# Ten FFN blocks with three Strassen-like pairs instead of two, B's stores on another queue, and two edits at the GLU

## The chip, the core and the metric

The kernel runs on one core of one Trainium2 chip, as one launch. The metric is the device time in microseconds (us) of one execution; the median of three runs is given, and one more execution was recorded by the hardware profiler.

## The reference

One decoder block on x of shape (1, 256, 2048), all in float32:

```python
u   = rms_norm(x)
p   = u @ w_in                       # q, k, v, ssm_in, gate_attn, gate_ssm
y_a = diff_attention(q, k, v)        # 8 heads, two softmax maps each
y_s = gelu(s5_scan(ssm_in))          # 64 groups, complex states
y_s = y_s * sigmoid(y_s @ w_glu + b_glu)
m   = sigmoid(g_a) * (y_a @ w_attn) + sigmoid(g_s) * (y_s @ w_ssm)
h   = x + rms_norm(m @ w_out)
z   = rms_norm(h)
f   = (silu(z @ w_gate) * (z @ w_up)) @ w_down     # 2048 -> 5632 -> 2048
out = h + rms_norm(f)
```

With 256 tokens the work is mostly the reading of weights and their products.

## The kernel before

A float32 product is made of three products in a rounded float32 type (fp32r): each operand is split into a high part and a low part (value minus high), and hi·hi, hi·lo and lo·hi are summed in PSUM. The tokens are two tiles of 128 (t = 0, 1). A weight matrix is read in k-tiles of 128 rows by 1024 columns: SyncE issues the load into a tile `raw`, ScalarE casts it to `hi`, VectorE subtracts to get `lo`; together this is a *split*. `ensure` emits splits up to 4 ahead of TensorE's products and loads further ahead. There are 3 + 2 buffers for hi and lo, so a buffer comes free after five sets. Nearly all vector, scalar and tensor instructions are recorded by one helper (line 41), which then puts them in a fixed order per engine; the order that results, not that of the code, is what each engine executes, in order and without overtaking.

The feed-forward part runs in blocks of 512 gate columns and 512 up columns. Block 0 is a plain block. Blocks 1 to 10 use a list `SETS`. An entry `D` is one k-tile: four partial products (P4, P5, P2, P3) into two 512-column banks, twelve matmuls of 128x512. A *quad* covers two k-tiles (k and k+1, a *pair*) by seven products instead of eight: entries `R2` (the second weight tile, 6 matmuls), `B1` (half of the first tile, 3), `T13` (two sums of weights, 6) and `T24` (two more, 6), so 21 matmuls where two `D` have 24. The sums of weights are made by `do_sums`, three VectorE subtractions: one 128x1024 (t1 and t3 together, called S13 below) and two 128x512 (t2, t4). The four loads of a pair go into one buffer, `ga[:, 1]`, and the sums into one buffer, `ga[:, 0]`. So in a trace a pair's work reads `ga<-ga` (sums) and `lo<-ga` (splits of R2, B1, T13, T24). `ensure` issues no loads of a next pair before the B1 split of the pair in hand has been emitted. The tokens' side of the seven products (sums of z) is made once by `combos` at the end of block 0. With two quads a block has 12 `D` and 2 quads, 186 matmuls.

Two other places matter. In the first part, the B matrices of the state space are made in `ga` and written to a scratch tensor `stack_b` in 12 stores of 256 KB (SyncE's queue, line 668); `fetch` (line 752) reads them back half a group at a time. GpSimd meanwhile builds tables of powers (lines 682 to 687). Where the GLU product begins, the last four gate banks of the input projection are evicted by `gs_evac` (three by ScalarE, one by VectorE), ScalarE casts y, loads an activation table, and TensorE starts on `w_glu`.

Of the kernel before, what the change touches and what calls it, by code (L numbers as in the profile page):

```python
# [14 lines left out]
ALU = mybir.AluOpType  # L15
# [74 lines left out]
def hybrid_block_kernel(  # L90
# [7 lines left out]
    nc = tc.nc  # L98
    pin = [True]
    V, A, T = (InOrder(tc, e, pin) for e in (nc.vector, nc.scalar, nc.tensor))  # L100
    G = nc.gpsimd
# [3 lines left out]
    stack_b = dram.tile([NG, 2, 3, 32, 2, 2, P], F32, name="stack_b")  # L105
# [37 lines left out]
    def big8(dtype=F32, shape=(P, 2048)):  # L143
        return b8.tile(list(shape), dtype, tag="b8", name=nm("b8"))
# [115 lines left out]
    def cap(blk, n, start=False):  # L260

        state["cap"] = None if n is None else blk.base + n
        if start:
            pin[0] = True
# [177 lines left out]
    hold = {}  # L442
# [76 lines left out]
    def prep():  # L519
# [57 lines left out]
        cs = pp.tile([P, 8, 32], F32, name="cs")  # L577
# [40 lines left out]
        for base, levels in ((0, 4), (4, 3)):  # L618
# [10 lines left out]
            for l in range(levels):  # L629
                n = 1 << l  # L630
# [20 lines left out]
        bh, bl = (ga[:, i, :, :].rearrange("p a (c o q) -> p (a c) o q", c=4, o=2) for i in range(2))  # L651
        for gg in range(NG // 2):
            ps = side()
            for e in range(2):
                g = 2 * gg + e
                for o in range(2):
                    t_ = blkB[e][o]
# [3 lines left out]
            gs = slice(2 * gg, 2 * gg + 2)  # L661
            src = ps.rearrange("p (a o q) -> p a o q", a=2, o=2)
            A.copy(bh[:, gs].bitcast(F32R), src)
            V.tensor_tensor(bl[:, gs], src, bh[:, gs], op=ALU.subtract)
            yield 0.7
        for n, t_ in enumerate((bh, bh, bl)):
            for j in range(4):
                nc.sync.dma_start(stack_b[:, j // 2, n, :, j % 2].rearrange("g q o n -> q g o n"), t_[32 * j:32 * j + 32])  # L668
                yield 0.2


    def table(hh):
# [291 lines left out]
    def scaled_copy(dst, src, sc):  # L964
        eng[0] += 1
        if eng[0] % 4:
            A.activation(dst, src, AF.Copy, scale=sc)
        else:
            V.tensor_scalar(dst, src, sc, None, op0=ALU.mult)
# [13 lines left out]
    def add(*a, **kw):  # L983
        b = Block(*a, **kw)
        if b.order is None:
            b.order = bank_order(b.nk)
        blocks.append(b)
        return b
# [24 lines left out]
    def first_load(k, r):  # L1013
# [6 lines left out]
        if k in (1, 3, 6):  # L1020
            load_x((1, 3, 6).index(k) + 1)

    tasks.append(("prep", prep()))
    add("ssm", 16, first_load, lx, proj_evac("u"), budget=1.2, ensure=x_ensure)

# [43 lines left out]
    def gs_evac(half_):  # L1069
        def f(key, accs):  # L1070
            t, c = key
            if ("gs", half_) not in hold:
                hold[("gs", half_)] = big8()
            scaled_copy(hold[("gs", half_)][:, t * 1024 + c * 512:t * 1024 + c * 512 + 512], accs[key],
                        hold["rstd"][:, t:t + 1])
        return f

    for hf in range(2):
# [2 lines left out]
    def gs_sigmoid(hf):  # L1081
        for c in (0, 1024):
            g = hold[("gs", hf)][:, c:c + 1024]
            A.activation(g, g, AF.Sigmoid)
# [21 lines left out]
    def glu_evac(key, accs):  # L1106
# [13 lines left out]
    add("glu", 8, load_std(w_glu, 0), None, glu_evac, mm=glu_mm, alloc=glu_alloc, pre=glu_pre,  # L1120
        order=[[(k, mt, 0) for mt in range(8)] for k in range(6)]
        + [[(k, mt, 0) for mt in (2 * b, 2 * b + 1) for k in (6, 7)] for b in range(4)], budget=0.6,
        before={2: lambda: gs_sigmoid(0), 4: lambda: gs_sigmoid(1), 6: lambda: cap(glu, 10, True)})
    glu = blocks[-1]

    def ly2(k, t):
# [37 lines left out]
    for hf in range(2):  # L1164
        add(f"ws{hf}", 8, load_std(w_ws, 1024 * hf), ly2, ws_evac(hf), budget=0.8, post=ws_post(hf),
            before={0: lambda: cap(glu, None), 1: unpin} if hf == 0 else None)
# [68 lines left out]
    def zf(t):  # L1235
        return ga[:, t].rearrange("p a (k n) -> p (a k) n", n=P)

    def combos(cb):

        if cb == 0:  # L1240
            cs = big8(F32R, (P, 2, 4, 2, P))
            hold["cs"], hold["cd"] = (cs[:, 0], cs[:, 1]), [big8(F32R, (P, 16, P)) for _ in range(2)]
        z0, z1 = zf(0), zf(1)
        n = 2 if cb % 2 else 4
        k0, k1, k2 = 4 * cb, 4 * cb + 2, 4 * cb + 3
        tt = V.tensor_tensor
        (ch, cl), (dh, dl) = hold["cs"], hold["cd"]
        tt(z1[:, k0:k0 + n], z0[:, k0:k0 + n], z1[:, k0:k0 + n], op=ALU.subtract)
        parts = [(z1[:, k0:k0 + n], dh[:, k0:k0 + n], dl[:, k0:k0 + n])]
        if n == 2:  # L1250
            tt(z1[:, k2], z1[:, k1], z1[:, k2], op=ALU.add)
            tt(z1[:, k1], z0[:, k1], z1[:, k1], op=ALU.subtract)
            tt(z0[:, k1], z1[:, k2], z0[:, k1], op=ALU.subtract)
            tt(z0[:, k2], z0[:, k2], z0[:, k1], op=ALU.subtract)
            parts += [(z1[:, k1:k1 + 2], ch[:, 0:2, cb // 2], cl[:, 0:2, cb // 2]),
                      (z0[:, k1:k1 + 2], ch[:, 2:4, cb // 2], cl[:, 2:4, cb // 2])]
        for src, h, l in parts:
            A.copy(h, src)
            tt(l, src, h.bitcast(F32), op=ALU.subtract)

    def h_transpose(t, cb):
        ps = side4()
        for j in range(4):
            k = 4 * cb + j
            transpose(ps[:, j * P:(j + 1) * P], hx[t][:, k * P:(k + 1) * P])
        z = zf(t)[:, 4 * cb:4 * cb + 4, :]
        V.tensor_tensor(z, ps.rearrange("p (a b) -> p a b", a=4),
                        wffn[:, 4 * cb:4 * cb + 4].unsqueeze(2).broadcast_to([P, 4, P]), op=ALU.mult)
        zs[t, cb] = z
# [26 lines left out]
    def norm2():  # L1296
# [9 lines left out]
        before={12: lambda: cap(wo1, 17, True), 13: lambda: cap(wo1, 17, True), 16: lambda: cap(wo1, 18), 17: lambda: h_transpose(0, 0)})  # L1306
# [6 lines left out]
    def load_ffn(b):  # L1313
        def f(k, r):
            for w, c0 in ((w_g, 0), (w_u, 512)):
                nc.sync.dma_start(r[:, :, c0:c0 + 512],
                                  w[k * P:(k + r.shape[1]) * P, b * 512:(b + 1) * 512].rearrange("(a p) c -> p a c", p=P))
        return f
# [33 lines left out]

    quad = lambda k: [(kind, k) for kind in ("R2", "B1", "T13", "T24")]
    plain = lambda *ks: [("D", k) for k in ks]
    SETS = plain(0, 1, 2, 3, 4) + quad(6) + plain(5, 8, 9, 10) + quad(14) + plain(11, 12, 13)
    USES = dict(D=(("P4", 0), ("P5", 1), ("P2", 0), ("P3", 1)), R2=(("P2", 0), ("P3", 1)), B1=(("P1", 0),),
                T13=(("P7", 1), ("P5", 0)), T24=(("P6", 0), ("P4", 1)))

    def s_mm(m, accs, h, l, first, last):
        n, key, c = m  # L1360
        kind, k = SETS[n]
        (ch, cl), (dh, dl) = hold["cs"], hold["cd"]
        z = lambda k_, t: tuple(zT[i][:, k_, t * P:(t + 1) * P] for i in "hl")
        q = k // 8
        if kind == "D":
            xh, xl = dict(P4=z(k, 1), P5=z(k, 1), P2=z(k, 0), P3=(dh[:, k], dl[:, k]))[key]
        elif key in ("P1", "P2", "P4"):
            xh, xl = dict(P1=z(k, 0), P2=z(k + 1, 0), P4=z(k + 1, 1))[key]
        else:
            i = dict(P7=0, P5=1, P6=2, P3=3)[key]  # L1370
            xh, xl = ch[:, i, q], cl[:, i, q]
        ps, sl = accs[key], slice(c * 512, c * 512 + 512)
        T.matmul(ps, xh, h[:, sl], start=first, stop=False)
        T.matmul(ps, xh, l[:, sl], start=False, stop=False)
        T.matmul(ps, xl, h[:, sl], start=False, stop=last)
# [17 lines left out]
    def s_evac(b):  # L1393
        def f(key, accs):
            s0, s1, X, Y = (hold["sc"][:, 512 * n:512 * n + 512] for n in range(4))
            plus = lambda o, a, k_: V.tensor_tensor(o, a, accs[k_], op=ALU.add)

            def gated(t, g, u):
                A.activation(g, g, AF.Silu, scale=hold["rstd2"][:, t:t + 1])
                V.scalar_tensor_tensor(g, u, hold["rstd2"][:, t:t + 1], g, op0=ALU.mult, op1=ALU.mult)  # L1400
                hid[(b, t)] = g
            if key == "P1":
                A.copy(s0, accs["P1"])
            elif key == "P6":
                plus(X, s0, "P6")
                plus(Y, X, "P7")
            elif key == "P4":
                plus(s1, Y, "P4")
            elif key == "P5":
                plus(X, X, "P5")  # L1410
                plus(Y, Y, "P5")
                gated(1, s1, Y)
            elif key == "P2":
                plus(s0, s0, "P2")
            elif key == "P3":
                plus(X, X, "P3")
                gated(0, s0, X)
                tasks.append((f"hid{b}", hid_t(b)))
        return f

    every = [[(n, key, c) for key, c in USES[kind]] for n, (kind, _) in enumerate(SETS)]
    s_order = [st[:3] for st in every[:3]] + [[st[3] for st in every[:3]]] + every[3:-2]
    s_order.append([st[i] for i in range(4) for st in every[-2:]])
    for b in range(1, NB):
        add(f"ffn{b}", len(SETS), load_ffn(b), None, s_evac(b), budget=0.6, mm=s_mm, alloc=s_alloc(b), order=s_order)
        blocks[-1].sets = SETS
        blocks[-1].akey = lambda m: m[1]
# [108 lines left out]
    def dn_weights():  # L1536
# [5 lines left out]
             before={8: dn_weights})  # L1542
# [39 lines left out]
```

## Time and profile before

| | us |
|---|---|
| median of three runs | 1394.79 |
| lowest, highest | 1393.06, 1396.41 |
| the profiled execution | 1398.8 |
| its span, first to last instruction | 1397.0 |
| TensorE busy in it | 1356.9 (97%) |
| VectorE busy | 1009.5 (72%) |
| ScalarE busy | 722.6 (52%) |
| GpSimd busy | 168.3 (12%) |

The mean granted TensorE clock was 0.983 of full speed. Busy shares are means over stages of different kinds. An instruction's length on VectorE overlaps the next by about 0.08 us, which is seen where two rows follow each other without idle time.

### The profile page before, as it was taken

What the parts mean: (1) busy time and instruction counts of PE and PEld (TensorE: products, weight loads), DVE (VectorE), ACT (ScalarE), POOL (GpSimd) and SP (SyncE); (2) the same over time, 40 slices, a digit from 0 to 9 for tenths busy, and PEclk for the clock granted to TensorE, in tenths of its full rate; (3) what the DMA queues carried; (4) which work ended last, traced back from release to release, by engine and by line L of the source; (5) the groups of instructions that cost most, each with busy time, mean ns of one, the idle gap of its engine ahead of it and who ended that gap; (6) DMA issues with size and microseconds to landing.
All of it is one profiled execution on the core that took longest, in us unless ns stands there. A gap on an engine that the chain in (4) does not pass through costs nothing.

```text
span 1397.0 us, 17778 instructions
## 1 busy us (share of the span) xinstructions
PE 1356.9 (97%) x6307; PEld 1104.5 (79%) x6307; DVE 1009.5 (72%) x1316; ACT 722.6 (52%) x1079; POOL 168.3 (12%) x187
## 2 busy tenths in 40 slices
PE   7999999999999989999999999999999999999997
PEld 6887777777777778888788888888888878888885
DVE  4954999868999956645976777767868676555555
ACT  3646545687545454544574555545555455444443
POOL 3090344302244100000000000000000000000001
PEclk8999999999999989999999999999999999999999
DMA  8678666544566556656566656566565566555551
GB/s 244 200 225 253 212 190 186 153 136 143 176 177 187 167 175 227 223 187 197 166 193 207 211 154 229 172 200 211 175 210 189 180 248 228 189 201 180 197 181 60
DMA packets 103577, 266.72 MB, mean 191 GB/s; under 512 B 11488, under 2 KB 18480, under 8 KB 100352
## 3 DMA queue, kind: packets, MB, share of 16 engines
q1 hardware_dynamic: 102272, 260.09, 58.5%
q10 hardware_dynamic: 608, 4.20, 0.8%
q0 software_dynamic: 608, 1.30, 0.4%
q8 instruction: 49, 0.80, 0.2%
q14 instruction: 40, 0.33, 0.1%
HBM read 257.16 MB, written 8.39 MB: 190 GB/s over the span
## 4 chain that ended last, share of the span: by engine, by line
issue 53%; PE 25%; DVE 13%; POOL 3%; ACT 3%; DMA 2%; SPq 1%; POOLq 0%; DVEq 0%; ACTq 0%
PE acc L41 23%; DVE lo L41 4%; PE side L41 2%; DVE ssB L41 2%; DVE ssD L41 2%; DVE ssA L41 2%; DVE ssC L41 1%; ACT hi L41 1%; DMA b<-in_x_dram 1%; SPq L668 1%; DVE ga L41 1%; DVE sim L41 1%; DVE b L41 1%; POOL tabS L685 1%; DVE sre L41 0%
## 5 line engine op out<-in xcount | busy, mean ns | idle before, releaser
L41 DVE TENSOR_TENSOR lo<-raw,hi 128x1024 fp32r<-128x1024 f32 (+1 forms) x385 | 473.6, 1240 | 163.7 <-ACT hi L41 163.0
L41 ACT CAST hi<-raw 128x1024 fp32r<-128x1024 f32 (+1 forms) x384 | 398.0, 1050 | 318.3 <-PE acc L41 220.1
L41 PE MATMUL acc<-hi,b 128*128 128x512 f32 x596 | 209.2, 394 | 0.4 <-DVE b L41 0.3
L41 PE MATMUL acc<-lo,xT_h 128*128 128x512 f32 x512 | 205.0, 404 | 2.6 <-DVE lo L41 2.5
L41 PE MATMUL acc<-hi,xT_l 128*128 128x512 f32 x512 | 202.4, 399 | 0.0
L41 PE MATMUL acc<-hi,xT_h 128*128 128x512 f32 x512 | 164.1, 406 | 5.3 <-ACT hi L41 3.5
L41 PEld LDWEIGHTS acc<-hi,b 128*128 128x128 f32 x596 | 112.4, 189 | 24.9 <-issue 0.8
L41 PEld LDWEIGHTS acc<-lo,xT_h 128*128 128x128 f32 x512 | 98.5, 193 | 28.1 <-DVE lo L41 5.1
L41 PEld LDWEIGHTS acc<-hi,xT_h 128*128 128x128 f32 x512 | 97.2, 193 | 28.4 <-ACT hi L41 6.2
L41 PE MATMUL acc<-lo,b 128*128 128x512 f32 x298 | 117.4, 394 | 2.1 <-DVE lo L41 2.1
L41 DVE TENSOR_TENSOR lo<-ga,hi 128x1024 fp32r<-128x1024 f32 x80 | 84.6, 1087 | 47.0 <-ACT hi L41 47.0
L41 ACT CAST hi<-ga 128x1024 fp32r<-128x1024 f32 x80 | 72.7, 943 | 82.1 <-PE acc L41 71.5
L41 PEld LDWEIGHTS acc<-hi,xT_l 128*128 128x128 f32 x512 | 98.3, 192 | 19.6
L41 PE MATMUL acc<-lo,zT_h 128*128 128x512 f32 x274 | 105.8, 392 | 0.4 <-DVE lo L41 0.4
L41 PE MATMUL acc<-hi,zT_l 128*128 128x512 f32 x274 | 105.1, 390 | 0.0
L41 PE MATMUL acc<-hi,zT_h 128*128 128x512 f32 x274 | 95.4, 393 | 0.2 <-ACT zT_h L41 0.2
L41 DVE TENSOR_TENSOR ga<-ga 128x512 f32<-128x512 f32 (+4 forms) x85 | 60.5, 716 | 35.4 <-DMA ga<-in_w_ffn_gate_dram 32.2
L439 POOL TENSOR_TENSOR rstdf<-rstdfm,half 128x1 f32<-128x1 f32 x2 | 1.1, 547 | 675.3 <-DVE rstdfm L41 675.3
L41 PE MATMUL side<-lo,zT_h 128*128 128x512 f32 x210 | 82.1, 391 | 0.0
L41 PE MATMUL side<-hi,zT_l 128*128 128x512 f32 x210 | 81.8, 389 | 0.0
L41 PE MATMUL side<-hi,zT_h 128*128 128x512 f32 x210 | 77.7, 389 | 0.0
L41 DVE TENSOR_TENSOR lo<-b,hi 128x1024 fp32r<-128x1024 f32 x40 | 49.0, 1225 | 39.0 <-ACT hi L41 39.0
(230 smaller groups left out, 2326.7 us busy)
## 6 DMA issues: line engine op xcount, KB each, us to landing
raw<-in_w_in_dram SPq DMA_DIRECT2D x127, 512.0 KB, 4.2
raw<-in_w_ffn_gate_dram SPq DMA_DIRECT2D x136, 256.0 KB, 3.7
raw<-in_w_ffn_up_dram SPq DMA_DIRECT2D x136, 256.0 KB, 4.0
raw<-in_w_ffn_down_dram SPq DMA_DIRECT2D x48, 512.0 KB, 4.3
b<-in_w_ffn_down_dram SPq DMA_DIRECT2D x20, 1024.0 KB, 4.9
raw<-in_w_out_dram SPq DMA_DIRECT2D x32, 512.0 KB, 4.1
ga<-in_w_ffn_gate_dram SPq DMA_DIRECT2D x40, 256.0 KB, 3.7
ga<-in_w_ffn_up_dram SPq DMA_DIRECT2D x40, 256.0 KB, 3.0
```

Source lines behind the costliest of these rows:

```text
L41: ins = f(*a, **kw)
L439: G.tensor_tensor(r, ms, half[:, :n], op=ALU.pow)
L668: nc.sync.dma_start(stack_b[:, j // 2, n, :, j % 2].rearrange("g q o n -> q g o n"), t_[32 * j:32 * j + 32])
L685: G.tensor_tensor(up(tss), hi(sa), lo(cb), op=ALU.mult)
```

## The change

Four parts. `SETS` has a third quad (k = 10), and the plain sets stand elsewhere; the tokens' sums for it are made by `combos` and kept in unused slots of another tile. The 12 stores of B go out on GpSimd's queue, in another sequence. `gs_evac` lets VectorE evict three of the last four gate banks. A `cap` delays the splits of `w_glu` in the first steps of the GLU block.

```diff
--- before.py
+++ after.py
@@ -663,10 +663,12 @@
             A.copy(bh[:, gs].bitcast(F32R), src)
             V.tensor_tensor(bl[:, gs], src, bh[:, gs], op=ALU.subtract)
             yield 0.7
-        for n, t_ in enumerate((bh, bh, bl)):
-            for j in range(4):
-                nc.sync.dma_start(stack_b[:, j // 2, n, :, j % 2].rearrange("g q o n -> q g o n"), t_[32 * j:32 * j + 32])
-                yield 0.2
+        for hf in range(2):
+            for n, t_ in enumerate((bh, bh, bl)):
+                for j in (0, 1):
+                    r = 32 * (2 * hf + j)
+                    G.dma_start(stack_b[:, hf, n, :, j].rearrange("g q o n -> q g o n"), t_[r:r + 32])
+                    yield 0.2
 
 
     def table(hh):
@@ -1071,8 +1073,12 @@
             t, c = key
             if ("gs", half_) not in hold:
                 hold[("gs", half_)] = big8()
-            scaled_copy(hold[("gs", half_)][:, t * 1024 + c * 512:t * 1024 + c * 512 + 512], accs[key],
-                        hold["rstd"][:, t:t + 1])
+            dst, sc = hold[("gs", half_)][:, t * 1024 + c * 512:t * 1024 + c * 512 + 512], hold["rstd"][:, t:t + 1]
+            if half_ == 1 and key != (0, 0):
+
+                V.tensor_scalar(dst, accs[key], sc, None, op0=ALU.mult)
+            else:
+                scaled_copy(dst, accs[key], sc)
         return f
 
     for hf in range(2):
@@ -1120,7 +1126,8 @@
     add("glu", 8, load_std(w_glu, 0), None, glu_evac, mm=glu_mm, alloc=glu_alloc, pre=glu_pre,
         order=[[(k, mt, 0) for mt in range(8)] for k in range(6)]
         + [[(k, mt, 0) for mt in (2 * b, 2 * b + 1) for k in (6, 7)] for b in range(4)], budget=0.6,
-        before={2: lambda: gs_sigmoid(0), 4: lambda: gs_sigmoid(1), 6: lambda: cap(glu, 10, True)})
+        before={0: lambda: cap(glu, 1), 1: lambda: cap(glu, 3), 2: lambda: (cap(glu, None), gs_sigmoid(0)),
+                4: lambda: gs_sigmoid(1), 6: lambda: cap(glu, 10, True)})
     glu = blocks[-1]
 
     def ly2(k, t):
@@ -1235,13 +1242,19 @@
     def zf(t):
         return ga[:, t].rearrange("p a (k n) -> p (a k) n", n=P)
 
+    def sums_of(k, i, n, part):
+
+        if k == 10:
+            return hold["cd"][part][:, (6, 7, 14, 15)[i]:(6, 7, 14, 15)[i] + n]
+        return hold["cs"][part][:, i:i + n, k // 8]
+
     def combos(cb):
 
         if cb == 0:
             cs = big8(F32R, (P, 2, 4, 2, P))
             hold["cs"], hold["cd"] = (cs[:, 0], cs[:, 1]), [big8(F32R, (P, 16, P)) for _ in range(2)]
         z0, z1 = zf(0), zf(1)
-        n = 2 if cb % 2 else 4
+        n = 2 if cb else 4
         k0, k1, k2 = 4 * cb, 4 * cb + 2, 4 * cb + 3
         tt = V.tensor_tensor
         (ch, cl), (dh, dl) = hold["cs"], hold["cd"]
@@ -1252,8 +1265,8 @@
             tt(z1[:, k1], z0[:, k1], z1[:, k1], op=ALU.subtract)
             tt(z0[:, k1], z1[:, k2], z0[:, k1], op=ALU.subtract)
             tt(z0[:, k2], z0[:, k2], z0[:, k1], op=ALU.subtract)
-            parts += [(z1[:, k1:k1 + 2], ch[:, 0:2, cb // 2], cl[:, 0:2, cb // 2]),
-                      (z0[:, k1:k1 + 2], ch[:, 2:4, cb // 2], cl[:, 2:4, cb // 2])]
+            for i, src in ((0, z1), (2, z0)):
+                parts.append((src[:, k1:k1 + 2], sums_of(k1, i, 2, 0), sums_of(k1, i, 2, 1)))
         for src, h, l in parts:
             A.copy(h, src)
             tt(l, src, h.bitcast(F32), op=ALU.subtract)
@@ -1352,7 +1365,8 @@
 
     quad = lambda k: [(kind, k) for kind in ("R2", "B1", "T13", "T24")]
     plain = lambda *ks: [("D", k) for k in ks]
-    SETS = plain(0, 1, 2, 3, 4) + quad(6) + plain(5, 8, 9, 10) + quad(14) + plain(11, 12, 13)
+    SETS = (plain(0, 1, 2, 3) + quad(6) + plain(4, 5) + quad(10) + plain(8, 9) + quad(14)
+            + plain(12, 13))
     USES = dict(D=(("P4", 0), ("P5", 1), ("P2", 0), ("P3", 1)), R2=(("P2", 0), ("P3", 1)), B1=(("P1", 0),),
                 T13=(("P7", 1), ("P5", 0)), T24=(("P6", 0), ("P4", 1)))
 
@@ -1361,14 +1375,13 @@
         kind, k = SETS[n]
         (ch, cl), (dh, dl) = hold["cs"], hold["cd"]
         z = lambda k_, t: tuple(zT[i][:, k_, t * P:(t + 1) * P] for i in "hl")
-        q = k // 8
         if kind == "D":
             xh, xl = dict(P4=z(k, 1), P5=z(k, 1), P2=z(k, 0), P3=(dh[:, k], dl[:, k]))[key]
         elif key in ("P1", "P2", "P4"):
             xh, xl = dict(P1=z(k, 0), P2=z(k + 1, 0), P4=z(k + 1, 1))[key]
         else:
             i = dict(P7=0, P5=1, P6=2, P3=3)[key]
-            xh, xl = ch[:, i, q], cl[:, i, q]
+            xh, xl = (sums_of(k, i, 1, part)[:, 0] for part in (0, 1))
         ps, sl = accs[key], slice(c * 512, c * 512 + 512)
         T.matmul(ps, xh, h[:, sl], start=first, stop=False)
         T.matmul(ps, xh, l[:, sl], start=False, stop=False)
```

On VectorE, in one of the FFN blocks before, around the second pair (first row: the split of R2; 852 is B1, 854 T13, 856 T24; 855 is S13 of the next pair, 851, 853, 857 and 859 are t2 and t4):

```order
850 L41 TENSOR_TENSOR lo_7616<-ga,hi_7615 128x1024
851 L41 TENSOR_TENSOR ga<-ga 128x512
852 L41 TENSOR_TENSOR lo_7635<-ga,hi_7634 128x512
853 L41 TENSOR_TENSOR ga<-ga 128x512
854 L41 TENSOR_TENSOR lo_7657<-ga,hi_7656 128x1024
855 L41 TENSOR_TENSOR ga<-ga 128x1024
856 L41 TENSOR_TENSOR lo_7676<-ga,hi_7675 128x1024
857 L41 TENSOR_TENSOR ga<-ga 128x512
858 L41 TENSOR_TENSOR lo_7696<-raw_7563,hi_7695 128x1024
859 L41 TENSOR_TENSOR ga<-ga 128x512
860 L41 TENSOR_TENSOR lo_7706<-raw_7576,hi_7705 128x1024
```

S13 of the next pair stands between this pair's T13 and T24.

The same engine after, from B1 of the first pair of a block (939) through T13 and T24, S13 of the second pair (942), two plain sets, that pair's R2, B1, T13 and t4 (946 to 949), to S13 of the third pair (950):

```order
939 L41 TENSOR_TENSOR lo_8211<-ga,hi_8210 128x512
940 L41 TENSOR_TENSOR lo_8234<-ga,hi_8233 128x1024
941 L41 TENSOR_TENSOR lo_8259<-ga,hi_8258 128x1024
942 L41 TENSOR_TENSOR ga<-ga 128x1024
943 L41 TENSOR_TENSOR lo_8275<-raw_8110,hi_8274 128x1024
944 L41 TENSOR_TENSOR lo_8285<-raw_8123,hi_8284 128x1024
945 L41 TENSOR_TENSOR ga<-ga 128x512
946 L41 TENSOR_TENSOR lo_8292<-ga,hi_8291 128x1024
947 L41 TENSOR_TENSOR lo_8302<-ga,hi_8301 128x512
948 L41 TENSOR_TENSOR lo_8322<-ga,hi_8321 128x1024
949 L41 TENSOR_TENSOR ga<-ga 128x512
950 L41 TENSOR_TENSOR ga<-ga 128x1024
```

Two plain sets instead of four stand between pairs. It goes on as follows, from R2 of the third pair (954) over B1 (956), T13 and T24 to S13 of the next block's first pair (960) and the block's last plain sets (961 and 963); rows 951 to 953, left out, are two plain sets and a T24:

```order
954 L41 TENSOR_TENSOR lo_8383<-ga,hi_8382 128x1024
955 L41 TENSOR_TENSOR ga<-ga 128x512
956 L41 TENSOR_TENSOR lo_8396<-ga,hi_8395 128x512
957 L41 TENSOR_TENSOR ga<-ga 128x512
958 L41 TENSOR_TENSOR lo_8413<-ga,hi_8412 128x1024
959 L41 TENSOR_TENSOR lo_8429<-ga,hi_8428 128x1024
960 L41 TENSOR_TENSOR ga<-ga 128x1024
961 L41 TENSOR_TENSOR lo_8445<-raw_8318,hi_8444 128x1024
962 L41 TENSOR_TENSOR ga<-ga 128x512
963 L41 TENSOR_TENSOR lo_8455<-raw_8337,hi_8454 128x1024
```

On SyncE before, the stores among the weight loads:

```order
53 L349 DMA raw_1194<-in_w_in_dram 128x1024
54 L349 DMA raw_1227<-in_w_in_dram 128x1024
55 L668 DMA stack_b<-ga 32x8x256 x12
56 L349 DMA raw_1229<-in_w_in_dram 128x1024
57 L349 DMA raw_1276<-in_w_in_dram 128x1024
58 L349 DMA raw_1311<-in_w_in_dram 128x1024
59 L752 DMA bsf_1177<-stack_b 96x512
```

and on GpSimd after, where they stand between a step of the tables and the next group's first:

```order
90 L689 TENSOR_TENSOR tabS_1213<-tabS_1213,tabt_209_1214 128x2x128
91 L685 TENSOR_TENSOR tabt_243_1359<-tabs_970,tabs_942 128x256
92 L670 DMA stack_b<-ga 32x8x256 x12
93 L687 TENSOR_TENSOR tabS_1358<-tabs_970,tabc_941 128x2x128
94 L684 TENSOR_TENSOR tabC_1357<-tabc_969,tabc_941 128x2x128
```

SyncE's loads close up over the gap, and GpSimd's next table step stands behind twelve stores.

On ScalarE before, at the start of the GLU product (presig is the activation after the table load; the first cast is y's first k-tile, the next `w_glu`'s, then the gate evictions):

```order
408 L41 ACTIVATE presig<-half 128x1
409 L41 CAST b_931_4609<-b_123_726 128x256
410 L41 CAST hi_4751<-raw_4649 128x1024
411 L41 ACTIVATE b_942_4665<-acc_4308,rstdx_608 128x512
412 L41 ACTIVATE b_942_4665<-acc_4309,rstdx_608 128x512
413 L41 ACTIVATE b_942_4665<-acc_4310,rstdx_608 128x512
414 L41 CAST b_931_4609<-b_123_726 128x256 x4
```

and after:

```order
406 L41 ACTIVATE presig<-half 128x1
407 L41 CAST b_931_4609<-b_123_726 128x256
408 L41 CAST hi_4779<-raw_4649 128x1024
409 L41 ACTIVATE b_942_4665<-acc_4308,rstdx_608 128x512
410 L41 CAST b_931_4609<-b_123_726 128x256 x4
411 L41 ACTIVATE b_942_4665<-b_942_4665 128x1024 x2
```

Two evictions leave ScalarE, and y's other four casts come right behind the first.

## Rows read from the trace of the kernel before

**Rows 1.** The page: busy time and share by engine

```profile
PE 1356.9 (97%) x6307; PEld 1104.5 (79%) x6307; DVE 1009.5 (72%) x1316; ACT 722.6 (52%) x1079; POOL 168.3 (12%) x187
```

**Rows 2.** Busy time by stretch: us, engines (instructions), TensorE clock, DMA share, GB/s

```profile
130.00:140.00 10.00, 7.03 (x24) 5.28 (x23) 2.45 (x2) 4.07 (x9) 0.00 (x0) 0.76 0.98 307
...
504.00:508.00 4.00, 3.12 (x14) 3.12 (x15) 2.98 (x6) 4.00 (x9) 0.00 (x0) 0.50 0.80 268
...
855.00:897.50 42.50, 42.50 (x189) 35.03 (x188) 32.37 (x35) 21.55 (x24) 0.00 (x0) 1.00 0.57 186
700.00:712.00 12.00, 12.00 (x55) 9.91 (x53) 10.14 (x18) 10.13 (x19) 1.64 (x1) 1.00 0.70 210
```

**Rows 3.** VectorE's groups by form, 855 to 1280 us: busy, mean ns, idle before

```profile
L41 DVE TENSOR_TENSOR lo<-raw,hi 128x1024 fp32r<-128x1024 f32 x111 | 133.8, 1221 | 32.2 <-ACT hi L41 32.0
...
L41 DVE TENSOR_TENSOR ga<-ga 128x512 f32<-128x512 f32 x26 | 17.9, 687 | 0.3
L41 DVE TENSOR_TENSOR b<-b,acc 128x512 f32<-128x512 f32 x27 | 17.6, 680 | 0.0
L41 DVE TENSOR_TENSOR ga<-ga 128x1024 f32<-128x1024 f32 x13 | 15.9, 1223 | 22.2 <-DMA ga<-in_w_ffn_gate_dram 22.2
...
L41 DVE SCALAR_TENSOR_TENSOR b<-b,rstdh 128x512 f32<-128x512 f32 x14 | 10.4, 745 | 0.0
```

**Rows 4.** VectorE's waits by what ended them: total us, times, longest

```profile
DVE ga L41 <- DMA ga<-in_w_ffn_gate_dram: 32.2, 13, 4.2
```

**Rows 5.** VectorE's timeline in one FFN block: start, us, [idle before]

```profile
857.22 4.10 DVE L41 TENSOR_TENSOR lo<-ga,hi 128x1024 fp32r<-128x1024 f32 x4 [5.49 <-ACT hi L41]
861.23 2.36 DVE L41 TENSOR_TENSOR lo<-raw,hi 128x1024 fp32r<-128x1024 f32 x2
863.51 1.22 DVE L41 TENSOR_TENSOR ga<-ga 128x1024 f32<-128x1024 f32 x1
...
868.65 0.68 DVE L41 TENSOR_TENSOR lo<-ga,hi 128x512 fp32r<-128x512 f32 x1
869.25 0.68 DVE L41 TENSOR_TENSOR ga<-ga 128x512 f32<-128x512 f32 x1
...
873.94 1.23 DVE L41 TENSOR_TENSOR ga<-ga 128x1024 f32<-128x1024 f32 x1 [2.56 <-DMA ga<-in_w_ffn_gate_dram]
```

**Rows 6.** TensorE's timeline: first product on the sums' low part

```profile
862.92 0.39 PE L41 MATMUL acc<-lo,b 128*128 128x512 f32 x1
```

**Rows 7.** SyncE's queue while B is stored

```profile
117.62 11.31 SPq L668 DMA_DIRECT2D stack_b<-ga  x12
129.03 2.80 SPq L349 DMA_DIRECT2D raw<-in_w_in_dram  x3
```

**Rows 8.** ScalarE's timeline in the same stretch

```profile
134.77 1.04 ACT L41 CAST hi<-raw 128x1024 fp32r<-128x1024 f32 x1 [8.95 <-DMA raw<-in_w_in_dram]
```

**Rows 9.** TensorE's timeline in the same stretch

```profile
135.87 2.07 PE L41 MATMUL acc<-hi,xT_h 128*128 128x512 f32 x4 [2.97 <-ACT hi L41]
```

**Rows 10.** GpSimd's timeline around the stores

```profile
105.49 0.63 POOL L683 TENSOR_TENSOR tabt<-tabs,tabs 128x256 f32<-128x256 f32 x1
154.98 2.67 POOL L685 TENSOR_TENSOR tabS<-tabs,tabc 128x256 f32<-128x256 f32 x1 [48.87 <-DVE ssB L41]
```

**Rows 11.** DMA issues of the first 60 us: KB, median us to landing

```profile
cn<-in_ssm_c_im_dram POOLq DMA_DIRECT2D x1, 256.0 KB, 12.6
```

**Rows 12.** ScalarE's timeline where the GLU product begins

```profile
499.18 1.99 ACT L41 CAST hi<-raw 128x1024 fp32r<-128x1024 f32 x2 [3.82 <-DMA raw<-in_w_glu_dram]
...
504.15 1.83 ACT L41 ACTIVATE b<-acc,rstdx 128x512 f32<-128x512 f32 x3
505.88 1.32 ACT L41 CAST b<-b 128x256 fp32r<-128x256 f32 x4
```

**Rows 13.** TensorE's timeline there

```profile
504.88 0.80 PE L41 MATMUL acc<-b,hi 128*128 128x256 f32 x2 [6.33 <-ACT b L41]
```

## The prediction

> **What bounds the kernel now.** I began with the busy table, where the reader is to see that TensorE is busy 97% of the span and VectorE 72% [rows 1]. Those are means. The change acts in FFN blocks 1 to 10, so next I took the stretches: a 42.5 us stretch of these blocks has TensorE busy throughout at full clock, with 189 matmuls, that is 0.225 us from start to start, and VectorE busy for 32.4 us, ScalarE for 21.6 [rows 2]. TensorE bounds there, and a matmul less is worth 0.225 us only as long as VectorE's splits arrive ahead of it. So the third view is VectorE's timeline, and the fourth its waits. They show that VectorE's margin is smaller than 72% says: its queue stands still for the loads of a pair, 13 times and 32.2 us in all [rows 4], because the first of the three sums (S13) sits at the head of the queue while splits that could run stand behind it.
>
> **The FFN blocks, TensorE's side.** Each block loses three matmuls (186 to 183): 10 × 3 × 0.225 = 6.8 us, if nothing else becomes late.
>
> **The FFN blocks, VectorE's side.** The pitch of an instruction is its mean less the 0.08 us that overlaps the next: a 128x1024 split or S13 1.22 − 0.08 = 1.14, a 128x512 subtraction 0.60, an eviction 0.60, a scaled eviction 0.67 [rows 3]. A plain set costs 1.14; a quad costs R2, T13 and T24 (3.42), B1 (0.60) and the sums (1.14 + 2 × 0.60), 6.36 together. Evictions are seven of 0.60 and two of 0.67 per block, 5.5. Before: 12 × 1.14 + 2 × 6.36 + 5.5 = 31.9 us, which agrees with the 32.4 measured. After: 10 × 1.14 + 3 × 6.36 + 5.5 = 36.0 us. TensorE needs 183 × 0.225 and some 0.7 us of transposes, 41.9. On that alone VectorE would fit in.
>
> What is added to it are the waits for loads. In the timeline, B1's split ended at 869.33 and t4 at 869.93, and the next pair's S13 started at 873.94 [rows 5]: 4.6 us after the one, 4.0 after the other. The single pair buffer cannot be refilled sooner, since these two read it last. So S13 waits for 4.6 us after the previous B1, or 4.0 after t4 if that is later, less whatever VectorE has to do in between. I go through the order after the change with that rule. Second pair: T13 and T24 lie between, 2.28 us, so it waits 2.3. Third pair: T13 and t4 come before it, and t4 directly, so it waits 4.0. Next block's first pair: after t4 come T13 and T24, so 1.7. Sum 8.0 us per block; all of it stands ahead of the next plain splits in the same queue. Checked on before, the rule gives 2.9 us (4.0 less one split) where 2.56 was measured [rows 5], so it reads a little high; 6.0 us is my low bound. Before has 32.2 us in ten blocks, 3.2 each. VectorE's block thus becomes 42 to 44 us against TensorE's 41.9: by capacity alone −0.6 to +1.4 us per block against 42.6 before.
>
> Capacity is the kinder of two bounds, as the sets aren't interchangeable: VectorE may run ahead only as far as there are buffers. At the first quad of a block its lead is small: the four splits that began at 857.22 came after 5.49 us of waiting on ScalarE's cast, which waits for a buffer, and the last of them (T24) ended at about 861.3, while TensorE first used it at 862.92 [rows 5, 6]. That is 1.6 us of lead. From there to the block's last plain set the order after the change has 17 instructions of 1.14 and 7 of 0.60, 23.6 us, and all three waits, 6.0 to 8.0: 29.6 to 31.6 us. TensorE does 3 + 6 + 6 + 24 + 21 + 24 + 21 + 12 = 117 matmuls in that stretch, 26.3 us. With a lead of 1.6 to 2.8 VectorE is late by 29.6 − 26.3 − 2.8 = 0.5 us to 31.6 − 26.3 − 1.6 = 3.7 us, once in each block, and TensorE waits for it. What is waited is not given back, because at the block's end the deferred products hold the buffers again. I take 2.4 us, a bit above the middle, as the waits go into a queue that also needs ScalarE's cast of each sum. Less the 0.7 us of matmuls a block gets longer by 1.7 us: +17 us for ten. The ends are (0.5 − 0.7) × 10 = −2 and (3.7 − 0.7) × 10 = +30.
>
> **B's stores.** Twelve issues hold SyncE's queue for 11.31 us, and the next weight load goes out at 129.03 [rows 7]. ScalarE's cast then waits 8.95 us for it [rows 8], TensorE stands 2.97 us [rows 9], and its clock falls to 0.76 in that stretch, where 24 matmuls took 7.03 us of busy time instead of 24 × 0.225 = 5.4 [rows 2]. So at most 2.97 + 1.6 = 4.6 us can be won. On the other side GpSimd is idle from 106 to 154.98 [rows 10], and there is room for the issues; but its own 256 KB loads took up to 12.6 us to land [rows 11], and the read-back of B stands in SyncE's queue ahead of later weight loads. If the stores land late, the same wait appears there: at worst the same 4.6 us again. I take −1.5, a third of what could be won.
>
> The share of the DMA engines was 0.98 in that stretch, at 307 GB/s [rows 2]: 12 stores of 256 KB are 3.1 MB, 10.2 us of that. The Trainium skill says (Trainium Kernel Development and Optimization, Key Constraints) that transfers issued from SyncE, ScalarE and GpSimd run on the same 16 engines and interleave, and that several issuers only save issue time. By that rule 11.31 us of issue would go and 10.2 us of transfer stay, and the gain would be about 1 us in place of my 1.5; the row with 0.98 agrees with it.
>
> **The GLU's start.** TensorE waits 6.33 us and starts at 504.88 [rows 13], when ScalarE's first gate eviction, begun at 504.15, is through [rows 12]. That eviction stays where it is, with the table load and the wait for the load of `w_glu` ahead of it. The two evictions that go to VectorE bring y's other four casts from 505.88 to about 504.7, but TensorE is busy without a break from 504.88 on (3.12 us of 3.12 at a granted clock of 0.50, the lower of its two levels, 1.2 GHz) [rows 2], so nobody waited for them. The later splits can bring the first ones forward by one, 1 us at most; three evictions in VectorE's row, 2 × 0.67 more, can push a low part back by 1.3. I take −0.3, with −1.2 and +1.3 as ends.
>
> **The tokens' sums.** Two casts and some six VectorE subtractions more at the end of block 0, about 2 to 3 us, where VectorE has 10.14 us of work in 12 [rows 2]. Cover is block 0's own lead; I take 0, with +2 at the other end.
>
> **Sum.** 17 − 1.5 − 0.3 + 0 = +15.2 us on the profiled execution's 1398.8, 1414.0. That execution lies 4.0 above the median of the runs, so 1410.
>
> **Rivals.** *TensorE stays the bound.* S13 may be waited for less than my rule says, as with 32.2 us in 20 pairs before (1.6 each): three pairs at 1.6 are 4.8, VectorE's block 40.8, below 41.9, and the path 28.4 against 26.3 + 2.8. Then −6.8 − 1.5 − 0.3 comes out, to −11.4 with all of the B stores' gain: 1383 to 1386, say 1386. For it speaks that the loads' wait is only reached if VectorE is ahead, and that a late VectorE waits less; against it, the small lead at each block's start.
>
> *It cancels.* VectorE's lateness is at the low end, 0.5 to 0.7 us per block, and eats the matmuls: 1398.8 − 1.5 − 0.3 ± 2 less 4.0, about 1393.
>
> *The stores on the other queue decide.* TensorE keeps its 6.8 us, but B comes back late, and SyncE stands at the read-back with weight loads behind it: no weight load can go out until the last store has landed, up to 12.6 us after its issue [rows 11]. Against the 2.97 us stop of before [rows 9] that is 9.6 us more, and 1.6 again at the low clock: 1398.8 − 6.8 + 11.2 − 4.0 = 1399. It decides from 6.8 us of added stop on. For it speaks the landing time; against it, that the read-back in SyncE's queue has moved behind more weight loads than before.
>
> **Chances and range.** Forecast 0.57 (1399 to 1428 by the ends of its terms, 1410 its middle); TensorE stays the bound 0.25; cancels 0.13; stores 0.05. A run of this kernel can tell 0.2%, about 2.8 us, from no change. The first rival is faster altogether; of the cancelling case about half is faster and half the same; the last and the forecast's cases are slower, but for a few at its low end that are the same. So faster 0.32, same 0.11, slower 0.57. The range is 1386 to 1428: up to the upper ends of the FFN term, and down to the first rival's value.
>
> **What would show it.** Right: in the FFN blocks VectorE's waits for the pair's loads grow from 32 to 60 us or more, TensorE shows idle time ended by VectorE's low parts (or ScalarE's casts of sums) once or more in each block, and a block lasts 44 us or so. Wrong: TensorE stays without gaps there and its blocks last 41.9 us. The stores' term is right if TensorE's gap at 133 us shrinks, wrong if one opens at the read-back of B. At the GLU the first product would start within 1 us of where it was, relative to the end of the input projection. A larger fall of the clock in the FFN blocks than 0.95 would make the time longer than my range.

## The result and the profile after

The changed kernel takes 1417.21 us (median; 1415.06 to 1420.61), the kernel before 1395.6 in the same comparison: ratio 1.0161, 95% interval 1.0145 to 1.0177, so 21.6 us slower. Forecast were 1410 and +15.2.

The page of the changed kernel, busy time by engine (it answers to [rows 1]):

```profile
PE 1361.3 (96%) x6277; PEld 1097.7 (77%) x6277; DVE 1050.6 (74%) x1374; ACT 737.1 (52%) x1099; POOL 175.9 (12%) x199
```

VectorE has 41 us more to do, TensorE 30 matmuls less, and yet its busy share has fallen. Where the time is: the ten FFN blocks, from the first matmul of block 1 to the last of block 10, first of before, then of the changed kernel (columns as in [rows 2]):

```profile
714.04:1149.50 435.46, 435.01 (x1958) 359.94 (x1956) 323.93 (x350) 223.32 (x255) 0.00 (x0) 1.00 0.60 196
```

```profile
713.79:1168.69 454.90, 439.81 (x1928) 355.22 (x1928) 364.65 (x400) 238.30 (x275) 0.00 (x0) 0.99 0.59 186
```

The blocks take 19.4 us longer, nearly all of the loss. TensorE is idle for 15.1 us of 454.9 where it was idle for 0.4 us before; the rest of the loss hides in matmuls that start more than 0.227 us after the one before them, while the engine counts as busy. I therefore lined up the matmuls of each trace with the program and counted, set by set, what TensorE's starts take beyond 0.2267 us each, the distance of starts where nothing is waited for. That sum is called *lost time* below: 0.1 us in before's ten blocks, 26.1 us in the changed kernel's (26.1 − 6.8 = 19.3, the difference above). Summed over the ten blocks, by place: 6.5 us in D0 to D2, 10.1 in D3, 9.2 from the second pair's T24 on (that T24 2.7, D8 2.1, D12 4.4). D3's 10.1 us lie in blocks 3, 5, 7 and 9 alone, 2.1 to 3.1 us in each. The profiled execution of before took 4.0 us more than its median, and at 50 us all the other profiles are 1.1 to 3.7 us ahead of it, so below only what is gained or lost between two places of a profile is compared.

VectorE's waits from 712 to 1161 us, changed kernel (answers to [rows 4], where the loads had 32.2 us in 13 waits):

```profile
DVE lo L41 <- ACT hi L41: 38.1, 27, 5.5
DVE ga L41 <- DMA ga<-in_w_ffn_gate_dram: 29.6, 17, 2.8
DVE b L41 <- PE side L41: 13.7, 4, 3.6
DVE ga L41 <- DMA ga<-in_w_ffn_up_dram: 3.7, 6, 1.5
```

The waits for a pair's loads are more in number, 23 instead of 14, but not longer in sum (33.3 us; before had 34.6 with the one on an up load). That contradicts my rule, though not the time.

Why the rule fails can be read at the end of block 9, VectorE in the changed kernel (t4 of the third pair, then the next block's S13):

```profile
1109.43 0.69 DVE L41 TENSOR_TENSOR ga<-ga 128x512 f32<-128x512 f32 x1
1110.27 1.23 DVE L41 TENSOR_TENSOR ga<-ga 128x1024 f32<-128x1024 f32 x1 [0.15 <-DMA ga<-in_w_ffn_up_dram]
```

S13 starts 0.15 us after t4 has ended, where the rule has 4.0. In `do_sums` t4 is the last to read the second tile's gate half, and S13 doesn't read this half, so it need not wait for the load that t4 lets go.

Two places in one block each. After t4 of the second pair, VectorE, then TensorE:

```profile
960.90 0.68 DVE L41 TENSOR_TENSOR ga<-ga 128x512 f32<-128x512 f32 x1
964.01 1.23 DVE L41 TENSOR_TENSOR ga<-ga 128x1024 f32<-128x1024 f32 x1 [2.42 <-DMA ga<-in_w_ffn_gate_dram]
965.15 1.22 DVE L41 TENSOR_TENSOR lo<-raw,hi 128x1024 fp32r<-128x1024 f32 x1
```

```profile
966.42 0.50 PE L41 MATMUL side<-lo,zT_h 128*128 128x512 f32 x1 [0.83 <-DVE lo L41]
```

S13 of the third pair waits 2.42 us at the head of the queue (the forecast had 4.0), the plain set D8 behind it is split too late, and TensorE stands 0.83 us. That is the mechanism of the forecast. D12 behind the third pair loses in the same way, behind S13 of the next block's first pair; VectorE, then TensorE, in block 8:

```profile
1066.95 1.23 DVE L41 TENSOR_TENSOR ga<-ga 128x1024 f32<-128x1024 f32 x1 [2.72 <-DMA ga<-in_w_ffn_gate_dram]
1068.09 1.22 DVE L41 TENSOR_TENSOR lo<-raw,hi 128x1024 fp32r<-128x1024 f32 x1
```

```profile
1069.37 0.50 PE L41 MATMUL side<-lo,zT_h 128*128 128x512 f32 x1 [0.90 <-DVE lo L41]
```

The other place is the entry of a block; TensorE, ScalarE and VectorE in the changed kernel at the start of block 5:

```profile
898.53 0.39 PE L41 MATMUL acc<-hi,zT_l 128*128 128x512 f32 x1
898.75 0.39 PE L41 MATMUL side<-hi,zT_h 128*128 128x512 f32 x1
...
899.89 0.39 PE L41 MATMUL side<-hi,zT_l 128*128 128x512 f32 x1
900.78 0.96 PE L41 MATMUL acc<-hi,zT_h 128*128 128x512 f32 x3 [0.50 <-ACT hi L41]
902.79 0.50 PE L41 MATMUL acc<-lo,zT_h 128*128 128x512 f32 x1 [1.05 <-DVE lo L41]
```

```profile
899.68 1.05 ACT L41 CAST hi<-raw 128x1024 fp32r<-128x1024 f32 x1 [1.98 <-PE side L41]
```

```profile
900.31 1.29 DVE L41 TENSOR_TENSOR b<-b,side 128x512 f32<-128x512 f32 x2 [3.39 <-PE side L41]
901.51 1.22 DVE L41 TENSOR_TENSOR lo<-raw,hi 128x1024 fp32r<-128x1024 f32 x1
```

Up to 898.53 these are products of the new block's D2; `side` from 898.75 to 899.89 are the last products of the old block's D12 and D13, and only they free the buffers that D3's split needs. The cast starts at 899.68, VectorE first adds a bank that the same products finished to two results (900.31), then splits (901.51), and TensorE waits 0.50 and 1.05 us. Before, the same products stand the other way round:

```profile
889.90 0.39 PE L41 MATMUL side<-hi,zT_h 128*128 128x512 f32 x1
...
891.03 0.39 PE L41 MATMUL side<-hi,zT_l 128*128 128x512 f32 x1
891.26 0.39 PE L41 MATMUL acc<-hi,zT_h 128*128 128x512 f32 x1
...
893.98 0.46 PE L41 MATMUL acc<-lo,zT_h 128*128 128x512 f32 x1
```

There the old products (`side`, 889.90 to 891.03) come ahead of D2 (891.26), D2's nine matmuls cover the split of D3, and nothing is lost. I had read this engine's order at neither place. The order is made by a scheduler; the helper of line 41 only holds the code's order where it is told to, which the description of the kernel should have said.

### The profile page after: what moved, and what is told of

The parts are those of the page before. It is cut to its first block, busy times and chain, and to the rows that moved or that the text cites. A ratio compares the mean times of both kernels' runs of the same rounds, so it can differ in the third digit from the quotient of the medians.

```text
span 1417.3 us, 17855 instructions
## 1 busy us (share of the span) xinstructions
PE 1361.3 (96%) x6277; PEld 1097.7 (77%) x6277; DVE 1050.6 (74%) x1374; ACT 737.1 (52%) x1099; POOL 175.9 (12%) x199
## 4 chain that ended last, share of the span: by engine, by line
issue 53%; PE 24%; DVE 11%; POOL 6%; ACT 2%; DMA 2%; SPq 0%; POOLq 0%; DVEq 0%; ACTq 0%
PE acc L41 22%; DVE lo L41 3%; PE side L41 2%; DVE ssB L41 2%; DMA raw<-in_w_in_dram 2%; POOL tabS L687 2%; DVE ssD L41 2%; DVE ssA L41 1%; ACT hi L41 1%; DVE ssC L41 1%; POOL tabC L684 1%; POOL tabC L686 1%; DVE b L41 1%; DVE ga L41 0%; POOL tabS L689 0%
## 5 line engine op out<-in xcount | busy, mean ns | idle before, releaser
L41 DVE TENSOR_TENSOR lo<-raw,hi 128x1024 fp32r<-128x1024 f32 (+1 forms) x365 | 449.1, 1237 | 158.7 <-ACT hi L41 158.0
L41 ACT CAST hi<-raw 128x1024 fp32r<-128x1024 f32 (+1 forms) x364 | 377.6, 1050 | 323.0 <-PE acc L41 226.8
L41 DVE TENSOR_TENSOR lo<-ga,hi 128x1024 fp32r<-128x1024 f32 (+1 forms) x120 | 126.9, 1088 | 34.9 <-ACT hi L41 34.7
L41 ACT CAST hi<-ga 128x1024 fp32r<-128x1024 f32 (+1 forms) x120 | 110.4, 942 | 79.4 <-DVE ga L41 29.2
L41 DVE TENSOR_TENSOR ga<-ga 128x512 f32<-128x512 f32 (+4 forms) x119 | 87.3, 738 | 34.4 <-DMA ga<-in_w_ffn_gate_dram 29.6
L41 PE MATMUL acc<-hi,zT_l 128*128 128x512 f32 x259 | 101.5, 396 | 0.0
L41 PE MATMUL acc<-hi,zT_h 128*128 128x512 f32 x259 | 89.1, 397 | 2.2 <-ACT hi L41 2.0
L41 PE MATMUL side<-lo,zT_h 128*128 128x512 f32 x195 | 76.6, 393 | 3.4 <-DVE lo L41 3.4
L41 PE MATMUL side<-hi,zT_l 128*128 128x512 f32 x195 | 76.1, 390 | 0.0
L41 PE MATMUL side<-hi,zT_h 128*128 128x512 f32 x195 | 73.6, 395 | 2.4 <-ACT hT L41 1.2
```

What stands on the lines that cost most here:

```text
L41: ins = f(*a, **kw)
```

## The experiments

Four ran first, to share out the loss and to test the wait.

**quad_only**: before with `SETS`, `combos` and `sums_of` of the change, all else as before.

> Third quad alone; B's stores and both GLU edits as before. If the whole loss sits in the FFN blocks (VectorE's row late for the splits): 1414 to 1420, FFN blocks 1 to 10 some 20 us longer than before (429 to about 449 us). If the other parts carry a share of the loss: under 1408.

1413.83 us, ratio 1.0140 (1.0118 to 1.0161), 0.2 us under the first range. Blocks 454.7 us, lost time 25.9 us at the same sets. The third pair alone makes 19.6 of the 21.6 us.

**rest_only**: the change with two quads and the old `SETS`.

> B's stores on GpSimd's queue and both GLU edits, with two quads as before. If the loss is the third quad's: 1390 to 1396, the stop of TensorE at 133 us gone (3 to 5 us won there), of which later stages may take some back. If the stores' move costs elsewhere: over 1400.

1396.24 us, ratio 1.0012 (1.0002 to 1.0022): 1.7 us slower by the ratio, and 0.2 us over the first range. TensorE's stop at 133 us is gone (windows of this kernel; before had 7.03 us busy in the second, [rows 2]):

```profile
120.00:130.00 10.00, 9.93 (x45) 7.75 (x43) 2.51 (x3) 2.37 (x3) 1.91 (x4) 1.00 1.00 320
130.00:140.00 10.00, 9.93 (x44) 7.97 (x43) 5.24 (x5) 6.20 (x11) 0.00 (x0) 1.00 0.93 323
```

Counted by matmul it gains 4.6 us on before between 130 and 140 us, and has given them back by 370 us. In between VectorE is busy nearly all the time, as it is in before (49.08 and 50.00 us of these 50):

```profile
150.00:200.00 50.00, 49.59 (x233) 38.52 (x232) 49.78 (x64) 25.27 (x39) 22.49 (x18) 1.00 0.64 190
200.00:250.00 50.00, 46.97 (x225) 35.77 (x224) 49.59 (x65) 23.37 (x35) 23.47 (x18) 1.00 0.64 190
```

**sums_still**: the sums read a tile that lies ready.

```diff
-        V.tensor_tensor(sums[:, 0:1024]..., pair[:, :, 1], pair[:, 0], op=ALU.subtract)
+        src = hx[0]
+        V.tensor_tensor(sums[:, 0:1024], src[:, 0:1024], src[:, 1024:2048], op=ALU.subtract)
...
```

> The changed kernel, but the three sums of a pair are made from x's residual tile, which lies ready, in place of the pair's weights (so the FFN's result is another); the same instructions on VectorE and the same loads, only no wait of the sums for the pair's loads. If those waits (33 us of VectorE's time) at the head of the queue make the splits late: 1396 to 1404. If VectorE's amount of work (36 us a block) decides: 1408 to 1415. If the five buffers of hi and lo decide: 1414 to 1418, no change.

1420.99 us, ratio 1.0188 (1.0168 to 1.0208): none of the three. By set it says more: the lost time at T24, D8 and D12 is gone in every block (9.2 to 0.0 us), that of D3 is unchanged (9.8), and about 13 us are lost in blocks 1 and 2, where the loads go out in another order: in block 2 SyncE's queue is held for 8.55 us by loads of pairs, ScalarE's cast waits 10.09 us for a plain set's load behind them, and TensorE stands 3.79 us. As a total it is inconclusive; by set the wait for the loads costs what was lost from the second pair's T24 on, and none of D3.

**sums_pool**: the three sums on GpSimd (`G.tensor_tensor`).

> The changed kernel with the three sums of a pair on GpSimd, so VectorE has 7.0 us less work in a block (36.0 to 29.0) and no wait for the pair's loads. If VectorE's row is the bound: 1387 to 1396. If GpSimd is too slow for it (over 8 us for a pair's sums, against 10.2 us of matmuls a quad and two plain sets have): over 1420, with ScalarE's casts of the sums waiting for GpSimd. If the buffers of hi and lo decide: 1412 to 1418.

1437.24 us, ratio 1.0306 (1.0285 to 1.0327). GpSimd's three took 2.9, 2.2 and 1.9 us, 7.0 per pair, under the 8 that I had named; but VectorE's splits beside it took 1.70 instead of 1.22 us [rows 3]:

```profile
L41 DVE TENSOR_TENSOR lo<-raw,hi 128x1024 fp32r<-128x1024 f32 x88 | 147.8, 1704 | 31.3 <-ACT hi L41 31.3
L41 DVE TENSOR_TENSOR lo<-ga,hi 128x1024 fp32r<-128x1024 f32 x63 | 95.6, 1543 | 8.3 <-ACT hi L41 8.2
```

VectorE was busier than with the sums (403.5 us in the blocks against 364.7), so this doesn't test what it was for. That it is over 1420, as the second case had it, has another reason than that case gave.

The next four took the candidates that were left: the pair buffer, the five buffers of hi and lo, the quad's place.

**pair2**: the pair's loads alternate between `ga[:, 1]` and `hT[:, 36:44]` (free until block 9), in blocks 1 to 8.

> The changed kernel with a second buffer for the pair's loads in blocks 1 to 8 (in a part of hT that is written only in blocks 9 and 10). TensorE's stalls in these blocks sum to 26 us, 9.2 of them after the second pair (its T24, D8 and D12), 16.2 in the first sets of a block. If the middle ones come from the single pair buffer: 1407 to 1410 and they are gone, those of the first sets stay. If the wait for the loads costs nothing: 1415 to 1419. If the load of the next pair can start so early that the first sets profit too: under 1402.

1406.19 us, ratio 1.0083 (1.0065 to 1.0101), in the first range. Lost time 14.4 us: from the second pair's T24 on 0.6 (from 9.2, and that in block 10, which has the single buffer), D3 still 10.0, D0 to D2 3.6 (from 6.5). So the single buffer cost 11.7 of the 26.1 us, 2.9 of them in the next block's first sets. VectorE's waits for the pair's loads fell to 2.8 us.

**b1own**: a small buffer of its own for a B1 set (`small1`), and splits five sets ahead.

```diff
...
+        if small1:
+            h = late["pool"].tile([P, 512], F32R, tag="b1h", name=nm("hi"), bufs=1)
+            l = late["pool"].tile([P, 512], F32R, tag="b1l", name=nm("lo"), bufs=1)
...
-        ahead = min(i + (4 if late ...
+        ahead = min(i + (5 if flat[i][0].sets else 4 if late ...
```

> The changed kernel with a small buffer of its own for B1's high and low part, so that a quad takes three of the five large ones instead of four, and splits emitted five sets ahead in the FFN blocks. (For the space, hT's high and low parts have two buffers in place of three.) If the first sets of a block stall because the buffers of the old block's last sets come free too late: 1401 to 1408, with the stalls at D3 down from 10.1 us to under 4. If VectorE's work and order decide there: 1414 to 1420.

1407.76 us, ratio 1.0093 (1.0072 to 1.0114). The time is in the range, the reason isn't: D3 still loses 9.4 us; the gain is from the second pair's T24 on (2.1 left) and in D0 to D2 (3.9), where the second pair buffer gains too. That the greater look-ahead does it, by meeting S13's wait earlier, is likely but not shown: no run has it without B1's own buffer.

**pair2_b1own**: both.

> Both together. If the two causes are separate and add up: 1392 to 1399. If VectorE's 36.0 us of work a block is the true bound behind them: 1406 to 1412. If either one alone already removes all that can be removed: as the better of the two.

1404.48 us, ratio 1.0071 (1.0051 to 1.0091): not additive, and nearest to the third case. 11.7 us are lost, 8.9 of them at D3. Neither cause is the one of D3.

**late_quad**: `SETS` with D0 to D4 ahead of the first quad and only D5 between first and second.

> The changed kernel with five plain sets ahead of the first quad, as before had, and one in place of two between first and second (D0-4, Q6, D5, Q10, D8, D9, Q14, D12, D13). If the quad's nearness to the block's start makes the first sets stall: 1403 to 1410, D3's stalls gone. If the pair buffer decides: 1419 to 1426, since first and second pair stand closer. If it is only VectorE's sum of work: 1415 to 1419.

1412.13 us, ratio 1.0128 (1.0111 to 1.0145), between the ranges. D3 loses 8.6 us, in blocks 3, 5, 7 and 9 as ever, so the quad's place isn't it either. Of what can be read at D3, TensorE's order, shown above, is left. The last four hold that order.

**pin_entry**: TensorE's products of a block's last two and first four sets in the code's order (in `s_mm`, `TK.matmul` stands for `T.matmul`), transposes behind the fourth set.

```diff
+    keep = [False]
+    TK = InOrder(tc, nc.tensor, keep)
...
+        keep[0] = n < 4 or n >= len(SETS) - 2
...
```

> The changed kernel with TensorE's products of a block's last two and first four sets held in the order of the code (the old block's last products ahead of the new block's first), and a block's transposes moved behind the next block's fourth set. In the changed kernel D2 of the new block runs ahead of the old block's last products, so that D3's split gets its buffer late. If that order makes the stalls at D0 and D3 (16 us): 1403 to 1408, D3's stalls under 2 us, those after the second pair still there. If the deferred buffers are needed anyway, or VectorE's work decides: 1413 to 1420, with the stalls only moved to other sets.

1435.87 us, ratio 1.0296 (1.0279 to 1.0314). D3 loses 0.0 us and D0 to D2 1.5, as the order theory had it, but 45.9 us are lost in D12 and D13. The second case had the stalls move to other sets; the time is over both ranges.

**pair2_pin**: the same with pair2.

> The same with a second buffer for the pair's loads in blocks 1 to 8. If pair buffer and order at the entry are the two causes, nearly all of the 26 us go: 1388 to 1394, under the kernel before. If VectorE's 36.0 us of work a block bound it: 1398 to 1406, with new stalls.

1416.36 us, ratio 1.0158 (1.0143 to 1.0174). D0 to D3 1.1 us, from the second pair's T24 to D9 nothing, but 21.3 in D12 and D13. This is over both ranges too.

**pair2_b1own_pin**: with b1own as well.

> The same with B1's own small buffer and splits five sets ahead as well. If the buffers of hi and lo still cost something once the order is held: 1 to 4 us less than without; otherwise the same within 2 us.

1407.73 us, ratio 1.0101 (1.0086 to 1.0116), 8.6 us less than without, more than either case had. 17.2 us are lost in D12 and D13, nearly all in even blocks. Here the cause can be read; TensorE, then VectorE, at the end of block 4:

```profile
883.47 0.39 PE L41 MATMUL side<-hi,zT_l 128*128 128x512 f32 x1
886.17 0.53 PE L41 MATMUL side<-hi,zT_h 128*128 128x512 f32 x1 [2.31 <-DVE b L41]
886.51 0.61 PE L41 MATMUL side<-lo,zT_h 128*128 128x512 f32 x1
...
888.20 0.63 PE L41 MATMUL side<-hi,zT_l 128*128 128x512 f32 x1
```

```profile
884.30 1.22 DVE L41 TENSOR_TENSOR lo<-raw,hi 128x1024 fp32r<-128x1024 f32 x1
885.44 0.68 DVE L41 TENSOR_TENSOR b<-b,side 128x512 f32<-128x512 f32 x1
```

At 883.47 the last product of P4 starts; P5's (886.17) go into the other half of the same double bank and wait 2.31 us until VectorE has evicted P4 (885.44, behind splits). In the changed kernel the scheduler puts the new block's D0 to D2 into that gap; held in order, nothing fills it. Only even blocks have P4 and P5 in one double bank, and D3 loses only in the odd blocks behind them (3, 5, 7, 9): the order at the entry and the shared bank belong together. After the stop the matmuls start up to 0.43 us apart.

**pair2_b1own_pin_bank**: in even blocks P4 shares its double bank with P3, and the first three sets put off P2.

```diff
...
-                d["P4"], d["P5"], d["P2"] = wide[:, 0, :], wide[:, 1, :], side()
-                for key in ("P1", "P6", "P7", "P3"):
+                d["P4"], d["P3"], d["P5"] = wide[:, 0, :], wide[:, 1, :], side()
+                for key in ("P1", "P6", "P7", "P2"):
...
+    e_order = [[st[0], st[1], st[3]] for st in every[:3]] + [[st[2] for st in every[:3]]] + s_order[4:]
...
```

> As pair2_b1own_pin, with another PSUM layout in even blocks: P4 shares its double bank with P3 in place of P5, and the new block's first three sets put off P2 in place of P3. In pair2_b1own_pin the only stall left, 3.4 to 4.1 us in each even block, is P5's products waiting for VectorE's eviction of P4 from the same double bank, then running at the lower clock. If the shared bank is the cause: those 16 us go to under 4, and the time is 1389 to 1395, at or under the kernel before. If VectorE's work of 36 us a block is the cause behind it: the stall moves to another eviction, and the time stays at 1403 to 1409.

1393.81 us, ratio 0.9995 (0.9986 to 1.0004): 23 us faster than the change, and level with before. The blocks in this kernel:

```profile
715.61:1144.31 428.70, 427.77 (x1922) 353.76 (x1921) 363.73 (x397) 238.85 (x269) 0.00 (x0) 1.00 0.61 193
```

428.7 us, 6.8 less than before, with VectorE as busy as in the slow version (363.7 us). About 1.2 us more than in before are still lost, at one wait in block 9; eight transposes of 0.11 us, which lie inside the window in before and in the changed kernel, stand ahead of it here. They turn block 0's result, and TensorE waits for VectorE ahead of them:

```profile
713.93 0.66 PE L41 MATMUL side<-ident,b 128*128 128x128 f32 x4 [1.59 <-DVE b L41]
715.20 0.66 PE L41 MATMUL side<-ident,b 128*128 128x128 f32 x4 [0.60 <-DVE b L41]
```

From the start of block 0's last product to block 1's first it is 3.65 us, in before 0.23. So of the 6.8 us 3.4 go at this seam and, by matmul counts, about 1 us more up to the GLU, where B's stores have moved. The medians differ by 0.9 us; the rest is not settled. No run changes the bank alone, or holds the order with the bank but without the added buffers, so what each of the four edits is worth by itself stays open.

## Why the prediction was right, and where it wasn't

- *30 matmuls, 6.8 us*: right, seen in the blocks of the last experiment but for about 1 us.
- *VectorE's work, 31.9 to 36.0 us a block*: right; 323.9 and 364.7 us in ten blocks.
- *S13's waits grow to 8.0 us a block*: wrong, 3.3. By pair: the second's S13 waits 0.2 us on average (forecast 2.3), the third's 1.6 (4.0), the next block's first 1.6 (1.7). The 4.0 us after t4 don't hold, as shown above: S13 doesn't read what t4 lets go. Nor do the 4.6 us after B1: second pairs' S13 start 2.8 to 3.3 us after it.
- *VectorE late by 2.4 us a block, on the way from the first quad to the last plain set*: the size was 2.6, but only 0.9 of it lies there (9.2 us in ten blocks, gone with a second pair buffer). The failed step is "once in each block" on that path: 1.7 us a block are lost ahead of it, in D0 to D3. Of these 0.3 go with the second buffer as well, and 1.0 are D3's, where an order of TensorE frees D3's buffer late, in blocks 3, 5, 7 and 9; most of the rest follows a wait at D2 of each even block for ScalarE's copy of the transposes. I counted the lead at the first quad and took the sets ahead of it as safe, because before showed no loss there.
- *VectorE becomes the bound*: not by its amount of work. With the same work, another order and layout and more buffers the blocks lose about 1 us. Order, shared banks and the single pair buffer made it late.
- *B's stores, −1.5 us*: locally 4 to 5 us were won, all that could be, and given back up to 370 us, mostly in a stretch where VectorE is busy 99% of the time. With the GLU edits the net is +1.7 us (interval +0.3 to +3.1). Why it is a loss and not zero stays open. By the rule that I quoted from the Trainium skill (Trainium Kernel Development and Optimization, Key Constraints), that several issuers only save issue time, my estimate was a gain of about 1 us. The measurement differs both ways: at the place itself the stop went altogether, as the weights no longer stood behind the stores in one queue, and in the total nothing was gained.
- *GLU, −0.3; tokens' sums, 0*: by matmul counts the distance of the changed kernel to before is −0.24 us ahead of the GLU's start (490 us) and −0.24 after it (520 us), and −0.25 at block 1's first product. In these two profiles both are worth nothing, within 0.1 us.

The time fell within the range through one right mechanism of less than half of the size (11.7 us with what the second buffer gains in D0 to D2, against 24 forecast) and one that I hadn't seen. That they add up to nearly the forecast is luck: the number is better than its reason.

## What to carry to other kernels

Before an engine with 80% is called the bound, look where TensorE loses time, set by set: the causes here were a single load buffer and a product order at the block's entry, behind which stood a bank shared by two results, and not the amount of work. Where a scheduler makes the order, read the order of the engine that bounds as well as that of the one that feeds it, above all at the seams between blocks. The stop that was removed ahead of a stretch in which VectorE is busy 99% of the time was worth nothing at the end.

## What the runs showed of the hardware

GpSimd and VectorE slow each other. With the sums on GpSimd, VectorE's 128x1024 split of loaded weights took 1.70 us on average instead of 1.22 (and still 1.22 where no sum ran beside it). Of GpSimd's sixty 128x512 subtractions the three that VectorE left alone took 1.29 us each, those beside VectorE's work 2.07 on average; GpSimd, then VectorE, which stands still from 846.75 to 851.30:

```profile
845.14 2.16 POOL L240 TENSOR_TENSOR ga<-ga 128x512 f32<-128x512 f32 x1
847.38 1.29 POOL L241 TENSOR_TENSOR ga<-ga 128x512 f32<-128x512 f32 x1
```

```profile
843.32 2.83 DVE L41 TENSOR_TENSOR lo<-raw,hi 128x1024 fp32r<-128x1024 f32 x1
846.07 0.68 DVE L41 TENSOR_TENSOR b<-b,side 128x512 f32<-128x512 f32 x1
```

A stop of TensorE of 2.31 us (pair2_b1own_pin) was followed by a granted clock of 0.83 over 10 us, with matmuls up to 0.43 us apart (the lower level, 1.2 GHz). Stops of 0.50 and 1.05 us within 2 us left it at 1.00 in the 6 us around them in block 5 of the changed kernel; in block 7 the same two stops were followed by 0.57 over 4 us, and in block 9 by 0.57 over 4 us too, so the length of a stop alone does not tell whether the clock falls:

```profile
882.00:892.00 10.00, 7.69 (x28) 5.87 (x27) 6.75 (x10) 2.46 (x4) 0.00 (x0) 0.83 0.67 219
```

```profile
898.50:904.50 6.00, 4.45 (x18) 3.03 (x17) 4.19 (x6) 1.99 (x2) 0.00 (x0) 1.00 0.20 56
...
991.50:995.50 4.00, 4.00 (x11) 3.17 (x12) 2.95 (x4) 0.00 (x0) 0.00 (x0) 0.57 0.54 157
```
